# First expert table whole, then the second in groups of 4, 8, 8, 8 and 4 chunks, under one VectorE budget

## The chip, the core and the metric

One core of one Trainium2 chip runs the whole program. The metric is device time in microseconds from start to end of one execution; the times given are medians over runs, and the profile is of one execution of its own.

## What is computed

A decoder block on 256 tokens of width 2048 in float32: retention and dilated attention, a memory cross-attention, and then a PEER layer, in which every token picks 16 experts of 16384 for each of 8 heads. Only the last layer matters here:

```python
def peer_ffn(h, w_q, subkeys, u_tab, v_tab):
    qh = (ht @ w_q).reshape(t, PEER_HEADS, 2, PEER_QUERY_DIM // 2)
    sc = jnp.einsum('thpd,hpnd->thpn', qh, subkeys).astype(jnp.float32)
    v_top, i_top = lax.top_k(sc, PEER_TOPK)
    ...
    c_val, c_idx = lax.top_k(combo, PEER_TOPK)
    ...
    e_idx = i1 * PEER_N_KEYS + i2
    gates = jax.nn.softmax(c_val, axis=-1)
    ...
    def expert_block(args):
        x_, i_, g_ = args
        u = u_tab[i_]
        a = jax.nn.gelu(jnp.einsum('td,tkd->tk', x_, u), approximate=False)
        return jnp.einsum('tk,tkd->td', a * g_, v_tab[i_])
```

`u_tab` and `v_tab` have 16384 rows of 2048 floats each, 134 MB a table.

## The kernel before

Weights stream through the core as **pieces** of 128 x 4 x 512 floats (1 MB each). SP loads a piece into `raw` (three buffers, L1134); ScalarE casts it to the fp32r high part `hi` (L1144) and VectorE subtracts for the low part `lo` (L1145); TensorE multiplies with both. This split runs two pieces ahead of the matmuls. There are 464 pieces; the last 256 are the PEER tables, 128 of `u` and 128 of `v`. 32 chunks of 512 experts make a table, 4 pieces a chunk.

For 192 of the 256 tokens the layer is computed densely: all activations against `u` (`u_chunk`, L206 to L208, L900, L901; 20 matmuls of 512 columns a piece), times a gate matrix that is zero outside of the chosen experts, times `v` (`v_group`, 20 matmuls a piece, L1002, L1003). For the last 64 tokens the chosen rows are gathered instead ("lanes"): 128 gathered tiles of `u` rows and 128 of `v` rows, each 128 x 1024 floats (0.52 MB), fetched by an indirect DMA that POOL issues (L824), dotted on VectorE (L835) and later added up with weights on VectorE (L853). A fetch is written three tiles ahead of its use.

Beside the stream run generators, each a background job that gives up control with `yield`:

- `route`: the top-16 searches (L655 to L659), the pairs, the index picks (L712 to L715), all on VectorE, for one block of tokens and then for the other. Then `gate_matrix`: 24 batches of 8 tokens. Each token needs a weighted one-hot row (L751) and a plain one-hot row (L753), both on VectorE, and their outer product on TensorE (L760), which ScalarE copies out (L761) and SP writes to DRAM (`G`).
- `lanes`: the gathered rows.
- `weigh`: reads a chunk of `G` and of the activations back, multiplies (L939, L951), transposes, and splits the result (L945, L946, L959, L960) for `v_group`.

What sets the order is `tick()`. It is called once after a piece, and twice in a `u` piece while `fine` is set, from the start of `u` to the end of `gate_matrix`. Each generator has a credit of its own: `FINE` = 1.5 units a tick in the fine part, `TICK` = 4 outside; a yield names the cost of what was written. `lanes` yields 0.8 of two fine ticks' credit, or of one coarse tick's, and so advances 1.25 tiles a piece whatever else runs.

The stream takes the first 20 chunks of `u` (`RUN_AHEAD`), and then, in turn, a group of two chunks of `v` (8 pieces) and two chunks of `u`, until `u` is used up. At the end of each group, for each of four column blocks, `evac` adds both PSUM banks to the result rows in two VectorE adds (L969, L971).

Of the kernel before, what the change touches and what calls it, by code (L numbers as in the profile page):

```python
# [28 lines left out]
TOPK = 16  # L29
N_EXP = N_KEYS * N_KEYS  # L30
N_CH = N_EXP // 512
RUN_AHEAD = 20
RAW_BUFS = 3
SPLIT_AHEAD = 2
N_UNITS = 30
LANES = slice(64, 128)
LOW = slice(0, 64)
TICK = 4.0
LANE_STEP = 0.8
ROWS_AHEAD = 3  # L40
FINE = 1.5

P2PI = 2.0 * math.pi

# [31 lines left out]
def block_kernel(ctx, tc, a, out):  # L76
# [34 lines left out]
    nc.vector.tensor_copy(iota, iota_i)  # L111
    ident = cp.tile([128, 128], F32, name="ident")
    nc.vector.tensor_scalar(ident, diag_i, 0.0, None, op0=OP.is_equal)
    nhalf = cp.tile([128, 16], F32, name="nhalf")
    nc.vector.memset(nhalf, -0.5)
    warm = cp.tile([128, 1], F32, name="warm")
# [6 lines left out]

    def tick():

        gain = FINE if fine[0] else TICK
        for g in list(active):
            credit[g] = min(credit[g], 0.0) + gain
            try:
                while credit[g] > 0.0:  # L130
                    credit[g] -= next(g) or gain
            except StopIteration:
                active.remove(g)

    credit = {}

    def add(g):
        active.append(g)
        credit[g] = 0.0
        return g  # L140

    def wait(cond):
# [10 lines left out]
    def call(fn):  # L153
        prog.append((None, fn))
# [506 lines left out]
    G_d = [dp.tile([128 - 64 * tb, N_EXP], F32, name=f"G{tb}") for tb in range(2)]  # L661
    g_done = []

    rt = [{}, {}]

    def route_top(n, tb):

# [52 lines left out]
    def route_gates(tb):  # L720
        yield
        yield
        ex, sel, uc = rt[tb]["g"]
        nc.scalar.activation(ex, ex, AF.Exp)
        su = sp.tile([128, 2, 8], F32, tag="gsum", name="gsum")
        nc.vector.tensor_reduce(su[:, 0], ex, axis=AX.X, op=OP.add)
        nc.vector.reciprocal(su[:, 1], su[:, 0])
        nc.vector.tensor_tensor(sel[:, 2], ex, bc(su[:, 1, :, None], [128, 8, 16]), op=OP.mult)
        yield
        if tb:  # L730
            add(lanes(uc[:, 0:3]))
# [3 lines left out]
        nc.scalar.copy(uc[:, 3:6], tp)  # L735
        rt[tb] = {"T": uc[:, 3:6]}
        yield

    def gate_matrix():

        prev = None
        for tb, t0 in [(1, t0) for t0 in range(0, 64, 8)] + [(0, t0) for t0 in range(0, 128, 8)] + [(None, None)]:
            cur = None
            if tb is not None:
                it = rt[tb]["T"]
                cur = unit([8, 128]), unit([8, 128])
                for i in range(8):
# [50 lines left out]
    def lanes(sel):  # L800
# [26 lines left out]
        def turn():  # L827
            return LANE_STEP * (2 * FINE if fine[0] else TICK)
# [12 lines left out]
        ys = [unit([2, 512]) for _ in range(2)]  # L841
        for n in range(4):
# [7 lines left out]
        for i in range(128):  # L850
            r = rows.pop(128 + i)
            y = ys[i % 2].rearrange("p a b -> p (a b)")
            nc.vector.scalar_tensor_tensor(y, r, coef[:, i // 2:i // 2 + 1], y, op0=OP.mult, op1=OP.add)  # L853
            del r
            fetch(128 + i + ROWS_AHEAD)
            yield turn()
        for q in range(2):
            z = unit([2, 512])
            nc.scalar.copy(z[LANES], ys[q][LOW])
# [51 lines left out]
    def weigh():  # L911
# [18 lines left out]
        yield  # L930
        load(0)
        for c in range(N_CH):
            while (c + 1 < N_CH and c + 1 not in ga) or c > 2 * v_at[0] + 3:
                yield
            if c + 1 < N_CH:
                load(c + 1)
            yield
            t = w.pop(c)
            nc.vector.tensor_mul(t[:, 1], t[:, 1], t[:, 0])  # L939
            yield  # L940
# [6 lines left out]
            A_T[c] = o  # L947
            if c % 2 == 0:
# [3 lines left out]
            yield  # L952
# [10 lines left out]
    def v_group(gi):  # L963
        accs = {}
        last = gi == N_CH // 2 - 1

        def evac(n, acc):
            r = x_rows[n]
            nc.vector.tensor_add(r[:, 0], r[:, 0], acc[0])  # L969
            if not last:  # L970
                nc.vector.tensor_add(r[:, 1], r[:, 1], acc[1])  # L971
                if gi == N_CH // 2 - 2:
# [3 lines left out]
                    wait(lambda: "ys" in sm)  # L976
                    nc.scalar.copy(r[LANES, 1], sm["ys"][n // 2][LANES, n % 2])
                return
            w = work([512])
            nc.scalar.copy(w[LOW], acc[1][LANES])  # L980
            nc.vector.tensor_add(r[LOW, 1], r[LOW, 1], acc[1][LOW])
# [6 lines left out]
                    nc.gpsimd.tensor_mul(y_rows[n][:, tb], r[:, tb], g_fin[n // 2][:, n % 2])  # L988

        for n in range(4):  # L990
            for c2 in range(2):
                def fn(hi, lo, n=n, c2=c2):
                    c = 2 * gi + c2
                    v_at[0] = gi
                    wait(lambda: c in A_T and gi in B_T)
                    if c2 == 0:
                        accs[n] = [bank("acc", [512]) for _ in range(2)]
                    ta, tb = A_T[c], B_T[gi][:, c2]
                    for k in range(4):
                        f, e = c2 == 0 and k == 0, c2 == 1 and k == 3  # L1000
                        mm3(accs[n][0], ta[:, 0, k], ta[:, 1, k], hi[:, k], lo[:, k], f, e)
                        nc.tensor.matmul(accs[n][1], tb[:, k], hi[:, k], start=f, stop=False)  # L1002
                        nc.tensor.matmul(accs[n][1], tb[:, k], lo[:, k], start=False, stop=e)  # L1003
                    if n == 3:
                        del A_T[c]
                        if c2:
                            del B_T[gi]
                    if c2 == 1:
                        evac(n, accs.pop(n))
                piece(a["v"][(gi * 4 + n) * 2 + c2], fn)  # L1010


    g_fin = {}
# [86 lines left out]
            yield from route_gates(tb)  # L1100
        yield from gate_matrix()
    call(lambda: add(route()))
    call(lambda: add(weigh()))
    call(lambda: add(lanes_in()))

    def side_by_side(kq):
# [14 lines left out]

    stream = [e for e in prog if e[0] is not None]
# [113 lines left out]
def _layout(inputs):  # L1236
# [15 lines left out]
        "v": g["peer_v"][0].reshape(N_CH // 2, 2, 4, 128, 4, 512).transpose(0, 4, 1, 3, 2, 5).reshape(-1, 128, 4, 512),  # L1252
    }
    r.update(_constants())
    return {k: np.ascontiguousarray(v) for k, v in r.items()}
# [15 lines left out]
```

## Time and profile before

| | us |
|---|---|
| median of 3 runs (2646.44 to 2647.83) | 2647.04 |
| profiled execution | 2646.55 |
| its span, first to last instruction | 2644.8 |
| last split ahead of the `u` table to the last split of all | 1226.67 to 2622.40 |

The span is what the instructions show; 1.75 us of the profiled execution lie outside of it. In the views below, "busy" is the time in which an engine had an instruction under way; the granted clock of TensorE is a share of its full speed; instructions are named by the line that records them. Consecutive VectorE instructions overlap by some 0.08 us, so that the distance between two starts, not the duration, is what one costs in a row.

### The profile page before, as it was taken

What the parts mean: (1) busy time and instruction counts of PE and PEld (TensorE: products, weight loads), DVE (VectorE), ACT (ScalarE), POOL (GpSimd) and SP (SyncE); (2) the same over time, 40 slices, a digit from 0 to 9 for tenths busy, and PEclk for the clock granted to TensorE, in tenths of its full rate; (3) what the DMA queues carried; (4) which work ended last, traced back from release to release, by engine and by line L of the source; (5) the groups of instructions that cost most, each with busy time, mean ns of one, the idle gap of its engine ahead of it and who ended that gap; (6) DMA issues with size and microseconds to landing.
All of it is one profiled execution on the core that took longest, in us unless ns stands there. A gap on an engine that the chain in (4) does not pass through costs nothing.

```text
span 2644.8 us, 29732 instructions
## 1 busy us (share of the span) xinstructions
PE 2524.7 (95%) x11426; PEld 2077.2 (79%) x11426; DVE 1964.3 (74%) x2446; ACT 1176.3 (44%) x1084; POOL 573.1 (22%) x361
## 2 busy tenths in 40 slices
PE   9999999999999999999977799999999999899998
PEld 7888888888888888888765577778777878777786
DVE  7566546777564344556989999789888989899976
ACT  6444334443454443445433344454444444344444
POOL 0211110001000000000022233354443445355001
PEclk9999999999999999999998899999999999999999
DMA  7555555566575544564676799999999999999874
GB/s 288 201 181 170 181 193 172 179 237 245 207 284 177 191 155 148 178 220 163 207 278 237 250 291 301 337 374 398 393 366 347 394 383 416 361 381 388 302 267 153
DMA packets 160142, 700.51 MB, mean 265 GB/s; under 512 B 15968, under 2 KB 40576, under 8 KB 101120
## 3 DMA queue, kind: packets, MB, share of 16 engines
q1 hardware_dynamic: 110352, 531.18, 56.5%
q0 software_dynamic: 42736, 154.85, 15.5%
q10 hardware_dynamic: 6912, 12.59, 1.3%
q8 instruction: 90, 1.47, 0.2%
q14 instruction: 52, 0.43, 0.0%
HBM read 666.01 MB, written 31.98 MB: 264 GB/s over the span
## 4 chain that ended last, share of the span: by engine, by line
PE 50%; DVE 20%; DMA 7%; issue 5%; ACT 3%; POOL 0%; SPq 0%; ACTq 0%; DVEq 0%; POOLq 0%
PE acc L207 13%; PE acc L208 13%; PE acc L206 13%; DVE lo L1145 8%; DMA raw<-in_v_dram 3%; DVE unit L835 2%; ACT hi L1144 2%; PE acc L1002 2%; PE acc L1003 2%; DVE unit L751 2%; DVE unit L753 1%; DMA raw<-in_u_dram 1%; PE acc L900 1%; PE acc L901 1%; DMA unit<-in_v_rows_dram,unit 1%
## 5 line engine op out<-in xcount | busy, mean ns | idle before, releaser
L1145 DVE TENSOR_TENSOR lo<-raw,hi 128x2048 fp32r<-128x2048 f32 (+1 forms) x464 | 1058.7, 2283 | 508.4 <-ACT hi L1144 502.3
L1144 ACT CAST hi<-raw 128x2048 fp32r<-128x2048 f32 (+1 forms) x464 | 877.7, 1900 | 658.6 <-PE acc L208 292.9
L207 PE MATMUL acc<-lo,unit 128*128 128x512 f32 x2688 | 1059.1, 394 | 34.1 <-DVE lo L1145 33.6
L206 PE MATMUL acc<-hi,unit 128*128 128x512 f32 x2688 | 1069.4, 398 | 15.9 <-ACT hi L1144 9.7
L208 PE MATMUL acc<-hi,unit 128*128 128x512 f32 x2688 | 1054.4, 392 | 0.0
L207 PEld LDWEIGHTS acc<-lo,unit 128*128 128x128 f32 x2688 | 510.2, 190 | 149.4 <-DVE lo L1145 47.9
L206 PEld LDWEIGHTS acc<-hi,unit 128*128 128x128 f32 x2688 | 510.0, 190 | 120.3 <-ACT hi L1144 12.2
L208 PEld LDWEIGHTS acc<-hi,unit 128*128 128x128 f32 x2688 | 509.5, 190 | 106.3
L824 POOL DMA_INDIRECT unit<-in_u_rows_dram,unit x128 | 226.1, 1766 | 379.1 <-DVE unit L835 173.2
L824 POOL DMA_INDIRECT unit<-in_v_rows_dram,unit x128 | 241.1, 1883 | 251.3 <-DVE unit L853 64.5
L900 PE MATMUL acc<-hi,unit 128*128 128x512 f32 x512 | 204.2, 399 | 0.0
L901 PE MATMUL acc<-lo,unit 128*128 128x512 f32 x512 | 203.6, 398 | 0.0
L1002 PE MATMUL acc<-hi,unit 128*128 128x512 f32 x512 | 200.6, 392 | 0.0
L1003 PE MATMUL acc<-lo,unit 128*128 128x512 f32 x512 | 200.4, 391 | 0.0
L853 DVE SCALAR_TENSOR_TENSOR unit<-unit 128x1024 f32<-128x1024 f32 x128 | 161.5, 1277 | 6.8 <-DMA unit<-xs 6.7
L835 DVE CUSTOM_DVE_ANT_0 unit<-unit 128x1024 f32<-128x1024 f32 x128 | 154.6, 1216 | 4.8 <-DMA unit<-in_u_rows_dram,unit 4.7
L900 PEld LDWEIGHTS acc<-hi,unit 128*128 128x128 f32 x512 | 99.2, 194 | 21.7
L901 PEld LDWEIGHTS acc<-lo,unit 128*128 128x128 f32 x512 | 99.0, 193 | 21.5
L1003 PEld LDWEIGHTS acc<-lo,unit 128*128 128x128 f32 x512 | 96.7, 189 | 20.6
L1002 PEld LDWEIGHTS acc<-hi,unit 128*128 128x128 f32 x512 | 96.7, 189 | 20.6
L760 PE MATMUL sm<-unit 128*128 128x128 f32 x384 | 62.9, 309 | 13.8 <-DVE unit L753 9.5
L338 POOL TENSOR_TENSOR unit<-work 128x512 f32<-128x512 f32 x20 | 37.8, 1888 | 176.4 <-DVE work L336 157.0
(233 smaller groups left out, 1435.8 us busy)
## 6 DMA issues: line engine op xcount, KB each, us to landing
raw<-in_u_dram SPq DMA_DIRECT2D x128, 1024.0 KB
raw<-in_v_dram SPq DMA_DIRECT2D x128, 1024.0 KB
raw<-in_w_in_dram SPq DMA_DIRECT2D x96, 1024.0 KB
raw<-in_w_kv_dram SPq DMA_DIRECT2D x32, 1024.0 KB
raw<-in_w_out_dram SPq DMA_DIRECT2D x16, 1024.0 KB
raw<-in_w_qm_dram SPq DMA_DIRECT2D x16, 1024.0 KB
raw<-in_w_om_dram SPq DMA_DIRECT2D x16, 1024.0 KB
raw<-in_w_pq_dram SPq DMA_DIRECT2D x16, 1024.0 KB
```

What stands on the lines that cost most here:

```text
L206: nc.tensor.matmul(acc, lh, rh, start=start, stop=False)
L207: nc.tensor.matmul(acc, lh, rl, start=False, stop=False)
L208: nc.tensor.matmul(acc, ll, rh, start=False, stop=stop)
L824: nc.gpsimd.indirect_dma_start(rows[i], None, t, bass.IndirectOffsetOnAxis(ap=ix[:, j // 2, j % 2:j % 2 + 1], axis=0))
L835: nc.vector.tensor_tensor_reduce(r, r, hn[i % 2].rearrange("p a b -> p (a b)"), 1.0, 0.0, OP.mult, OP.add, dots[:, i // 2, i % 2:i % 2 + 1])
L853: nc.vector.scalar_tensor_tensor(y, r, coef[:, i // 2:i // 2 + 1], y, op0=OP.mult, op1=OP.add)
L900: nc.tensor.matmul(accs[1], th[:, k, 128:256], hi[:, k], start=first, stop=False)
L901: nc.tensor.matmul(accs[1], th[:, k, 128:256], lo[:, k], start=False, stop=last)
L1002: nc.tensor.matmul(accs[n][1], tb[:, k], hi[:, k], start=f, stop=False)
L1003: nc.tensor.matmul(accs[n][1], tb[:, k], lo[:, k], start=False, stop=e)
L1144: nc.scalar.copy(hi[:, ks], raw[:, ks])
L1145: nc.vector.tensor_sub(lo[:, ks], raw[:, ks], hi[:, ks])
```

## The change

- The stream takes all 32 chunks of `u` first and then `v` in five groups of 4, 8, 8, 8 and 4 chunks. The input `v` is laid out in that order. A group of 8 holds its two PSUM banks over 8 pieces for each column block, and there are 5 times 4 evacuations in place of 16 times 4. `hf_T` is given up at the end of `u`.
- `tick()` has one budget for all generators in the PEER part, to its end: 1.3 units, twice a piece, in `u` and in `v`. Generators are served by rank: `route` (and `lanes_in`) first, then `weigh`, then `lanes`. Lanes cost 1.28 units a tile, a half batch of one-hots 1.1, the steps of `weigh` 0.7 to 0.8.
- The plain one-hots go from VectorE to ScalarE, as Relu(1 - (iota - index) squared): eight Squares of 128 columns and one Relu of 1024 a batch. The indices are kept negated, and the weighted one-hots on VectorE compare with a negated iota.
- The chunk limit of `weigh` follows the chunks that are used up, 3 ahead in `u` and 9 ahead in `v`. The copy of `ys` moves to the last group.

```diff
-RUN_AHEAD = 20
+V_GROUPS = (4, 8, 8, 8, 4)
...
-LANE_STEP = 0.8
...
-FINE = 1.5
+BUDGET = 1.3
...
+        if fine[0]:
+            left[0] = min(left[0], BUDGET) + BUDGET
+            for g in sorted(active, key=lambda g: rank.get(g, 0)):
+                try:
+                    while left[0] > 0.0:
+                        cost = next(g)
+                        if not cost:
+                            break
+                        left[0] -= cost
+                except StopIteration:
+                    active.remove(g)
+            return
...
-                    nc.vector.tensor_scalar(cur[0][:, i], iota, it[:, 0, t], it[:, 2, t],
+                    nc.vector.tensor_scalar(cur[0][:, i], niota, it[:, 0, t], it[:, 2, t],
                                             op0=OP.is_equal, op1=OP.mult)
-                    nc.vector.tensor_scalar(cur[1][:, i], iota, it[:, 1, t], None, op0=OP.is_equal)
+                    nc.scalar.activation(cur[1][:, i], iota, AF.Square, bias=it[:, 1, t])
+                    if i % 4 == 3:
+                        yield 1.1
+                nc.scalar.activation(cur[1], cur[1], AF.Relu, scale=-1.0, bias=rt["one"])
...
-            yield 2.6
-        fine[0] = False
+            yield 0.1
...
-            yield turn()
+            yield 1.28
...
-            while (c + 1 < N_CH and c + 1 not in ga) or c > 2 * v_at[0] + 3:
+            while (c + 1 < N_CH and c + 1 not in ga) or c > v_at[0] + (3 if hf_T[0] is not None else 9):
...
+            wait(lambda: "ys" in sm)
+            nc.scalar.copy(r[LANES, 1], sm["ys"][n // 2][LANES, n % 2])
...
-    for c in range(RUN_AHEAD):
+    for c in range(N_CH):
         u_chunk(c)
-    for gi in range(N_CH // 2):
-        if gi == N_CH // 2 - 1:
+    def end_u():
+        hf_T[:] = [None] * 4
+    call(end_u)
+    c0 = 0
+    for gi, count in enumerate(V_GROUPS):
+        if gi == len(V_GROUPS) - 1:
             call(load_g_final)
-        v_group(gi)
-        for c in range(RUN_AHEAD + 2 * gi, min(RUN_AHEAD + 2 * gi + 2, N_CH)):
-            u_chunk(c)
+        v_group(gi, c0, count)
+        c0 += count
```

Three places show what this makes of the order. On VectorE, the beginning of one piece in the routing of the second token block, before (L1145 is the split of a piece; a top-16 search is the five rows from MAX to MAX_INDEX; L835 is the dot of one gathered tile, in two rows):

```order
L1145 TENSOR_TENSOR lo<-raw,hi 128x2048
L655 MAX unit<-unit 128x8
L656 MAX_INDEX unit<-unit 128x8
L657 MATCH_REPLACE work<-unit 128x128
L658 MAX unit<-work 128x8
L659 MAX_INDEX unit<-unit,work 128x8
L835 ISA unit<-unit 128x1024
L835 ISA unit 128x1
```

The same routing with the change, from one split to the next:

```order
L1172 TENSOR_TENSOR lo<-raw,hi 128x2048
L672 MAX unit<-unit 128x8
L673 MAX_INDEX unit<-unit 128x8
L674 MATCH_REPLACE work<-unit 128x128
L675 MAX unit<-work 128x8
L676 MAX_INDEX unit<-unit,work 128x8
L1172 TENSOR_TENSOR lo<-raw,hi 128x2048
```

The dot is gone from between the splits; the searches stay.

On ScalarE, two pieces in the building of the gate matrix, before (L1144 is the cast of a piece, L761 copies the products of four tokens):

```order
L1144 CAST hi<-raw 128x2048
L761 COPY unit<-sm 128x512 x2
L1144 CAST hi<-raw 128x2048
L761 COPY unit<-sm 128x512 x2
```

The same with the change (L774 Square of one token, L777 Relu of eight, L785 the copies):

```order
L1171 CAST hi<-raw 128x2048
L774 ACTIVATE unit<-iota,unit 128x128 x8
L777 ACTIVATE unit<-unit,one 128x1024
L785 COPY unit<-sm 128x512 x2
L774 ACTIVATE unit<-iota,unit 128x128 x4
L1171 CAST hi<-raw 128x2048
```

Eight to twelve Squares and a Relu came in beside each cast; on VectorE eight to twelve one-hots a piece remain.

On VectorE, two pieces some 80 pieces into the tables, before (L969 and L971 are the evacuation of a group's column block):

```order
L1145 TENSOR_TENSOR lo<-raw,hi 128x2048
L969 TENSOR_TENSOR unit<-unit,acc 128x512
L971 TENSOR_TENSOR unit<-unit,acc 128x512
L835 ISA unit<-unit 128x1024
L835 ISA unit 128x1
L1145 TENSOR_TENSOR lo<-raw,hi 128x2048
L835 ISA unit<-unit 128x1024
L835 ISA unit 128x1
```

The same place with the change:

```order
L1172 TENSOR_TENSOR lo<-raw,hi 128x2048
L855 ISA unit<-unit 128x1024
L855 ISA unit 128x1
L855 ISA unit<-unit 128x1024
L855 ISA unit 128x1
L1172 TENSOR_TENSOR lo<-raw,hi 128x2048
```

Two gathered tiles stand between two splits in place of 1.25 on average, and the evacuations are gone from there.

## Rows read from the trace of the kernel before

**Rows 1.** Page, part 1: busy us of each engine, share of the span, instructions.
```profile
PE 2524.7 (95%) x11426; PEld 2077.2 (79%) x11426; DVE 1964.3 (74%) x2446; ACT 1176.3 (44%) x1084; POOL 573.1 (22%) x361
```

**Rows 2.** Windows, five stages: us, busy PE, PEld, DVE, ACT, POOL, granted clock, DMA, GB/s.
```profile
1226.67:1543.58 316.91, 263.94 (x1099) 207.64 (x1098) 285.50 (x633) 129.76 (x111) 56.85 (x39) 0.92 0.69 239
1543.58:1723.77 180.19, 163.28 (x800) 136.24 (x799) 164.18 (x402) 79.43 (x83) 64.57 (x31) 0.93 0.95 309
1723.77:2001.82 278.05, 265.29 (x1168) 217.27 (x1166) 239.47 (x252) 128.82 (x96) 123.41 (x72) 0.98 0.99 378
2001.82:2433.38 431.56, 416.74 (x1857) 340.52 (x1856) 398.51 (x320) 193.07 (x140) 214.42 (x114) 0.99 1.00 387
2433.38:2622.40 189.02, 187.18 (x846) 153.79 (x844) 155.07 (x133) 93.77 (x78) 15.22 (x11) 1.00 0.75 266
```

**Rows 3.** Windows of the split L1145 alone, first and fourth stage: DVE busy (count).
```profile
1226.67:1543.58 316.91, 109.64 (x48) 0.92 0.69 239
...
2001.82:2433.38 431.56, 201.30 (x88) 0.99 1.00 387
```

**Rows 4.** Timeline of VectorE, one piece in the gate matrix: start, us, line.
```profile
1550.56 2.28 DVE L1145 TENSOR_TENSOR lo<-raw,hi 128x2048 fp32r<-128x2048 f32 x1
1552.76 0.33 DVE L751 TENSOR_SCALAR unit<-iota,unit 128x128 f32<-128x128 f32 x1
1553.02 0.27 DVE L753 TENSOR_SCALAR unit<-iota,unit 128x128 f32<-128x128 f32 x1
...
1556.38 1.21 DVE L835 CUSTOM_DVE_ANT_0 unit<-unit 128x1024 f32<-128x1024 f32 x1
...
1557.52 2.27 DVE L1145 TENSOR_TENSOR lo<-raw,hi 128x2048 fp32r<-128x2048 f32 x1
```

**Rows 5.** Timeline of TensorE, one batch of the gate matrix and the piece behind.
```profile
1547.46 2.57 PE L760 MATMUL sm<-unit 128*128 128x128 f32 x16
1549.79 0.48 PE L206 MATMUL acc<-hi,unit 128*128 128x512 f32 x1
...
1552.17 0.39 PE L206 MATMUL acc<-hi,unit 128*128 128x512 f32 x1
...
1553.30 0.39 PE L206 MATMUL acc<-hi,unit 128*128 128x512 f32 x1
```

**Rows 6.** Groups by line: busy us, mean ns of one, idle before.
```profile
L1144 ACT CAST hi<-raw 128x2048 fp32r<-128x2048 f32 x460 | 875.6, 1911 | 658.6 <-PE acc L208 292.9 <-DMA raw<-in_v_dram 148.0 <-DMA raw<-in_u_dram 73.0
L761 ACT COPY unit<-sm 128x512 f32<-128x512 f32 x48 | 27.7, 587 | 54.4 <-PE sm L760 49.7 <-issue 4.2 <-ACT unit L878 0.4
...
L261 ACT ACTIVATE unit<-unit 128x1024 f32<-128x1024 f32 x8 | 8.5, 1057 | 5.8 <-DMA unit<-in_x_dram 5.8
...
L432 ACT ACTIVATE work<-sm 128x128 f32<-128x128 f32 x16 | 4.3, 279 | 1.4 <-POOL unit L338 1.4
...
L824 POOL DMA_INDIRECT unit<-in_v_rows_dram,unit x128 | 241.1, 1883 | 251.3 <-DVE unit L853 64.5 <-PE tp L943 52.0 <-PE tp L955 47.6
```

**Rows 7.** Windows of 50 and of 10 us with the most DMA traffic.
```profile
2200.00:2250.00 50.00, 50.00 (x222) 41.39 (x221) 44.26 (x30) 24.94 (x17) 28.99 (x17) 1.00 1.02 417
...
1760.00:1770.00 10.00, 10.00 (x46) 8.28 (x45) 9.18 (x11) 5.19 (x3) 7.67 (x4) 1.00 1.02 420
2100.00:2110.00 10.00, 10.00 (x47) 8.26 (x47) 10.00 (x9) 4.23 (x3) 3.38 (x3) 1.00 1.01 404
```

**Rows 8.** Timeline of POOL, and of VectorE at the last of them.
```profile
2049.27 0.94 POOL L824 DMA_INDIRECT unit<-in_v_rows_dram,unit  x1 [0.30 <-issue]
...
2057.66 3.94 POOL L824 DMA_INDIRECT unit<-in_v_rows_dram,unit  x1 [0.66 <-DVE unit L853]
...
2058.50 2.28 DVE L1145 TENSOR_TENSOR lo<-raw,hi 128x2048 fp32r<-128x2048 f32 x1
```

**Rows 9.** Waits, who for whom: us, times, longest; third stage, then 1900:2000.
```profile
ACT hi L1144 <- DMA raw<-in_v_dram: 37.2, 11, 8.1
...
DVE unit L853 <- DMA unit<-xs: 6.7, 1, 6.7
```

More of the change, by code (lines that the diff above doesn't have):

```diff
@@ L113, in block_kernel @@
     nc.vector.tensor_scalar(ident, diag_i, 0.0, None, op0=OP.is_equal)
+    niota = cp.tile([128, 128], F32, name="niota")
+    nc.vector.tensor_scalar(niota, iota_i, -1.0, None, op0=OP.mult)
     nhalf = cp.tile([128, 16], F32, name="nhalf")
@@ L124, in tick, with add @@
     def tick():
-        gain = FINE if fine[0] else TICK
+        if fine[0]:
[10 more added lines that the diff above has]
+            return
         for g in list(active):
-            credit[g] = min(credit[g], 0.0) + gain
+            credit[g] = min(credit[g], 0.0) + TICK
             try:
                 while credit[g] > 0.0:
-                    credit[g] -= next(g) or gain
+                    credit[g] -= next(g) or TICK
             except StopIteration:
                 active.remove(g)
+    left = [0.0]
+    rank = {}
     credit = {}
-    def add(g):
+    def add(g, later=0):
         active.append(g)
         credit[g] = 0.0
+        rank[g] = later
         return g
@@ L662, in block_kernel @@
     g_done = []
-    rt = [{}, {}]
+    rt = {0: {}, 1: {}}
     def route_top(n, tb):
@@ L730, in route_gates @@
         if tb:
-            add(lanes(uc[:, 0:3]))
+            add(lanes(uc[:, 0:3]), 2)
         tp = bank("tp", [3, 128])
@@ L734, in route_gates @@
             nc.tensor.transpose(tp[:, s], uc[:, s], ident)
-        nc.scalar.copy(uc[:, 3:6], tp)
+        nc.scalar.activation(uc[:, 3:5], tp[:, 0:2], AF.Copy, scale=-1.0)
+        nc.scalar.copy(uc[:, 5], tp[:, 2])
+        if tb:
+            rt["one"] = cp.tile([128, 1], F32, name="one")
+            nc.vector.memset(rt["one"], 1.0)
         rt[tb] = {"T": uc[:, 3:6]}
@@ L825, in fetch @@
                     ap=ix[:, j // 2, j % 2:j % 2 + 1], axis=0))
-        def turn():
-            return LANE_STEP * (2 * FINE if fine[0] else TICK)
         for i in range(ROWS_AHEAD):
@@ L855, in lanes @@
             fetch(128 + i + ROWS_AHEAD)
-            yield turn()
+            yield 1.28
         for q in range(2):
@@ L939, in weigh @@
             nc.vector.tensor_mul(t[:, 1], t[:, 1], t[:, 0])
-            yield
+            yield 0.7
             tp = bank("tp", [4, 128])
@@ L947, in weigh @@
             A_T[c] = o
+            yield 0.7
             if c % 2 == 0:
@@ L951, in weigh @@
             nc.vector.tensor_mul(t[:, 1], t[:, 1], t[:, 0])
-            yield
+            yield 0.7
             tp = bank("tp", [4, 128])
@@ L961, in weigh, with v_group @@
             B_T[c // 2] = o
-    def v_group(gi):
+            yield 0.8
+    def v_group(gi, c0, count):
         accs = {}
-        last = gi == N_CH // 2 - 1
+        last = gi == len(V_GROUPS) - 1
         def evac(n, acc):
@@ L971, in evac @@
                 nc.vector.tensor_add(r[:, 1], r[:, 1], acc[1])
-                if gi == N_CH // 2 - 2:
+                if gi == len(V_GROUPS) - 2:
                     w = work([512])
@@ L975, in evac @@
                     nc.vector.tensor_add(r[LOW, 1], r[LOW, 1], w[LOW])
-                    wait(lambda: "ys" in sm)
-                    nc.scalar.copy(r[LANES, 1], sm["ys"][n // 2][LANES, n % 2])
                 return
+            wait(lambda: "ys" in sm)
+            nc.scalar.copy(r[LANES, 1], sm["ys"][n // 2][LANES, n % 2])
             w = work([512])
@@ L990, in v_group, with fn @@
         for n in range(4):
[L991 to L995, printed above, removed]
+            for c2 in range(count):
+                def fn(hi, lo, n=n, c=c0 + c2, c2=c2):
+                    wait(lambda: c in A_T and c // 2 in B_T)
                     if c2 == 0:
                         accs[n] = [bank("acc", [512]) for _ in range(2)]
-                    ta, tb = A_T[c], B_T[gi][:, c2]
+                    ta, tb = A_T[c], B_T[c // 2][:, c % 2]
                     for k in range(4):
-                        f, e = c2 == 0 and k == 0, c2 == 1 and k == 3
+                        f, e = c2 == 0 and k == 0, c2 == count - 1 and k == 3
                         mm3(accs[n][0], ta[:, 0, k], ta[:, 1, k], hi[:, k], lo[:, k], f, e)
@@ L1003, in fn @@
                         nc.tensor.matmul(accs[n][1], tb[:, k], lo[:, k], start=False, stop=e)
+                        if k == 1:
+                            tick()
                     if n == 3:
                         del A_T[c]
-                        if c2:
-                            del B_T[gi]
-                    if c2 == 1:
+                        v_at[0] += 1
+                        if c % 2:
+                            del B_T[c // 2]
+                    if c2 == count - 1:
                         evac(n, accs.pop(n))
-                piece(a["v"][(gi * 4 + n) * 2 + c2], fn)
+                piece(a["v"][4 * c0 + n * count + c2], fn)
     g_fin = {}
@@ L1102, in block_kernel @@
     call(lambda: add(route()))
-    call(lambda: add(weigh()))
+    call(lambda: add(weigh(), 1))
     call(lambda: add(lanes_in()))
@@ L1251, in _layout @@
         "u": g["peer_u"][0].reshape(N_CH, 512, 4, 4, 128).transpose(0, 2, 4, 3, 1).reshape(-1, 128, 4, 512),
-        "v": g["peer_v"][0].reshape(N_CH // 2, 2, 4, 128, 4, 512).transpose(0, 4, 1, 3, 2, 5).reshape(-1, 128, 4, 512),
+        "v": np.concatenate([
+            g["peer_v"][0][512 * c0:512 * (c0 + n)].reshape(n, 4, 128, 4, 512).transpose(3, 0, 2, 1, 4).reshape(-1, 128, 4, 512)
+            for c0, n in zip(np.cumsum((0,) + V_GROUPS), V_GROUPS)]),
     }
```

## The prediction

> **What bounds the kernel now.** I read the busy sums first [rows 1]: TensorE is busy 95% of the span, so the kernel looks bound by it. The sum hides five different stages, so I cut the PEER part by the splits of its 256 pieces [rows 2, 3] into 48, 24, 56, 88 and 40 pieces. A piece is 20 matmuls of 512 columns. Two L206 with five matmuls from the one to the other start 1.13 us apart in a run without gaps [rows 5], 0.227 us a matmul, so a piece needs 4.53 us of TensorE. What each stage gets:
>
> - Stage A (routing, first gate batches): 316.9 us for 48 pieces, 6.6 us each. VectorE is busy 285.5 us of it, TensorE 263.9 at a granted clock of 0.92, that is, partly at 1.2 and mostly at 2.4 GHz after gaps [rows 2]. VectorE sets the pace.
> - Stage B (most of the gate matrix): 180.2 us for 24 pieces, 7.5 us each. In its core a piece takes 6.97 us on VectorE without a gap: the split, eight pairs of one-hots, a dot [rows 4]. TensorE is nearly as full: a batch of the gate matrix takes it 2.33 us [rows 5], with a piece's 4.53 us that is 6.86.
> - Stages C and D (56 and 88 pieces, with the gathered tiles): 4.97 and 4.90 us a piece. TensorE is busy 95 and 97%, the DMA share is 0.99 and 1.00 at 378 and 387 GB/s [rows 2]. ScalarE's casts wait for loads here, 37 us in stage C for pieces of `v` alone [rows 9], though mostly within the two pieces of lead.
> - Stage E (40 pieces, gathered tiles nearly done): 4.73 us a piece, TensorE busy 99% [rows 2]. It is TensorE's own pace.
>
> **The change, part by part.** I go stage by stage; the order shows that the same 48, 24, 56, 88 and 40 pieces keep the routing, the gate matrix and the gathered tiles in the same stages, only with other numbers of them.
>
> Stage A. The order has 33 dots and 5 batches of one-hots there before, and 3 dots and no batch with the change; the routing is the same. A dot costs VectorE 1.14 us from start to start (1556.38 to 1557.52), a pair of one-hots 0.45 (3.62 us from 1552.76 to 1556.38 for eight) [rows 4]. VectorE loses 30 x 1.14 = 34 us and 40 x 0.45 = 18 us. 316.9 - 52 = 265 us stays above TensorE's 48 x 4.53 = 218 plus some 6 of transposes and scores, so VectorE still sets the pace and all of it counts: **-52 us**. If half of the remaining 31 us of VectorE's idle time grows, because the waits between softmax and transposes are no longer filled with dots, it is -40.
>
> Stage B. All 24 batches are in it now (19 before), and no dot until its end. VectorE needs 2.2 + 9 x 0.26 = 4.5 us a piece and is out of the way. TensorE needs 24 x 4.53 + 24 x 2.33 = 165 us. ScalarE takes over the plain one-hots: no row has a Square with these operands, the nearest is L432 with 0.279 us for 128 columns; the Relu is like L261, 1.057; two copies at 0.587 [rows 6]. 8 x 0.279 + 1.057 + 1.174 = 4.46 us a batch, 107 for 24; casts 24 x 1.91 = 46, the evacuations of six chunks some 11 (three instructions of 512 columns each, about 0.6 apiece): 164 us, as much as TensorE. These are durations, and starts stand a little closer, so TensorE is the bound by a small margin. Before, no engine was busy for more than 164 of the 180 us [rows 2]; with two engines equally full I take 175: **-5 us**, from -12 (TensorE alone) to +15 (Squares at 0.35).
>
> Stages C and D. What leaves VectorE: 88 of 124 evacuation adds, 53 us at about 0.6 (a quarter of the split's 2.2 and a start), but mostly where TensorE is busy 95 to 99%. What comes: the tiles that stage A and B had. Stage C gets 108 tiles instead of 69, stage D 135 instead of 110. The traffic: a piece is 1.049 MB, a tile 0.524, a chunk of activations written 0.39 on average, a chunk of `weigh` 0.52 plus half as much for the last tokens. Stage C before: 58.7 + 36.2 and 8 of the rest = 103 MB, and 103 MB in 278 us is 370 GB/s, which agrees with the view's 378. With the change: 58.7 + 56.6 + 8.2 = 123.5 MB. Stage D before: 165 MB (383 GB/s, the view 387); with the change 92.3 + 70.8 + 21.2 = 184.3 MB. The highest 10 us windows show 420 GB/s, and 417 is held for 50 us with a DMA share of 1.02 [rows 7]: I read this as the ceiling. Two tiles and a piece are 2.1 MB; at 417 GB/s that is 5.03 us, more than TensorE's 4.53 and than VectorE's 2.2 + 2 x 1.14 + 0.15 = 4.65. So **DMA becomes the bound of both stages**. I take 412 GB/s, near the rows at 404 to 420: C = 123.5 / 0.412 = 300 us, **+22**; D = 184.3 / 0.412 = 447, and 7 for the turn to the `v` rows, which waits for `xs` now [rows 9] and will again: 454, **+23**. At 420 the two are +16 and +14; at stage D's own 387, taken as the most that a mix can have, +41 and +52.
>
> The Trainium skill has two other figures for this ceiling ("DMA: Bandwidth & Descriptors", Specifications): about 358 GB/s from HBM to one core, and 435 for the fabric. By 358 the two stages would take 860 us, 150 more than now, and the kernel would be slower; the trace does not agree, since 50 us at 417 stand there [rows 7]. By 435 they would cost some 5 us, estimated from that page.
>
> Stage E. 6 tiles instead of 14, 88 fewer adds in all, none of it on TensorE's path: 40 x 4.53 and a few transposes is 186 of 189: **-3**.
>
> Costed at nothing: the negated iota and the constant (two small VectorE instructions, ahead of work that waits for loads or in the routing), the split copy in `route_gates` (one more ScalarE instruction, twice), the layout of `v` (same size, contiguous as before), the chunk limit of `weigh` (by the order, each chunk's parts stand 8 or more pieces ahead of their first use, 40 us). The `ys` copy stands now in the last group, ahead of the last sums: about 0.6 us of ScalarE in the tail, **+1**.
>
> Sum: 2644.8 - 52 - 5 + 22 + 23 - 3 + 1 = 2630.8 us of span, 2632.5 with the 1.75 us around it, and the medians lie 0.5 above the profiled run: **2633 us**, 0.5% faster.
>
> **The rivals.**
>
> *No DMA ceiling.* If the plateau at 417 is only demand, VectorE sets the pace in C and D: by the order's counts, 262 and 419 us of VectorE work, with 2% and the turn 267 and 434: -11 and +2. The sum is 2645 - 52 - 5 - 11 + 2 - 3 + 1 = 2577 of span, 2579 as a median. For it: TensorE is at full pace in the very windows at 417. Against it: the flat top, with a share of 1.02.
>
> *POOL cannot issue two tiles a piece (slower).* An indirect DMA takes POOL 0.94 us alone and 3.94 when it meets VectorE's long instructions: it ends 0.82 us after the split at 2058.50 has ended [rows 8]. The mean is 1.88, 2.18 with the 0.30 between two [rows 6, 8], and 16 tiles in 8 pieces need 35 us of 43. It decides from 2.67 us a tile. VectorE is denser in two-input instructions with the change; if each tile took 3.2 us (2.9 and 0.3), stage C would take 108 x 3.2 = 346 us, 46 more than forecast, and the 65 tiles of D's dense stretches 208 instead of 164: 2633 + 90 = 2723. The Trainium skill says why ("SBUF — State Buffer", Terms: VectorE and GpSimd lock a shared port pair for a whole instruction, the loser blocks); the trace agrees.
>
> *ScalarE is late in stage B.* Its 164 us become 187 if a Square takes 0.40 us: with 5% on top 196, +16 instead of -5, 2654, a little slower.
>
> **How the numbers follow.** About 0.2%, 5 us, can be told from no change here. Forecast (DMA ceiling between 395 and 420; the kernels are equal at about 403): 0.67, of which 0.48 faster, 0.09 the same, 0.10 slower. No ceiling: 0.14, faster. POOL: 0.11, slower. ScalarE: 0.08, half the same, half slower. Faster 0.62, same 0.13, slower 0.25. The range goes from 2574, which takes in the no-ceiling case, to 2680, which takes in 387 GB/s (2679) and the milder half of POOL's case.
>
> **What would show it.** Stage A at 260 to 275 us with no L855 between the searches, and a granted clock above 0.92. Stage B at 168 to 190 with TensorE and ScalarE both above 85%. Stages C and D at 405 to 420 GB/s with TensorE below 90% busy, dots or casts waiting for DMA. If they run at 4.7 us a piece with more than 425 GB/s, the ceiling is wrong; if POOL is busy throughout and DMA below 390, POOL is the bound; if stage A does not fall, something other than VectorE paced it.

## The result, and the profile after

The changed kernel takes 2736.74 us (median of 4, 2736.20 to 2740.41), the kernel before 2646.74 beside it: a ratio of 1.0347, 95% interval 1.0329 to 1.0365. It is **3.5% slower**; the forecast was 2633 us, faster, with a range to 2680. Both its sign and its range were wrong.

The busy sums of the page, part 1 (busy us, share of the span, instructions), beside [rows 1]:

```profile
PE 2541.2 (93%) x11426; PEld 2083.6 (76%) x11426; DVE 1880.1 (69%) x2168; ACT 1254.9 (46%) x1302; POOL 541.5 (20%) x361
```

VectorE has 84 us less to do, as the change wants, and the kernel is 90 us longer. The five stages, cut at the same splits as in [rows 2] (us; busy PE, PEld, DVE, ACT, POOL; granted clock, DMA share, GB/s):

```profile
1226.75:1498.39 271.64, 244.59 (x1041) 195.19 (x1040) 232.92 (x494) 128.94 (x114) 7.98 (x8) 0.97 0.62 212
1498.39:1682.35 183.96, 159.11 (x842) 137.33 (x841) 114.54 (x234) 157.53 (x297) 7.36 (x5) 0.93 0.81 249
1682.35:1985.35 303.00, 276.23 (x1166) 219.57 (x1165) 266.41 (x297) 136.71 (x106) 181.10 (x112) 0.98 1.00 399
1985.35:2516.40 531.05, 444.49 (x1900) 353.68 (x1899) 427.74 (x359) 191.34 (x144) 237.06 (x134) 0.94 0.93 350
2516.40:2710.45 194.05, 186.86 (x810) 153.87 (x809) 119.14 (x77) 90.53 (x69) 12.00 (x9) 0.97 0.64 227
```

| stage, us | before | forecast | after |
|---|---|---|---|
| A, routing | 316.9 | 265 | 271.6 |
| B, gate matrix | 180.2 | 175 | 184.0 |
| C, tiles in `u` | 278.1 | 300 | 303.0 |
| D, tiles in `v` | 431.6 | 454 | 531.1 |
| E, end of `v` | 189.0 | 186 | 194.1 |

A is 7 us late and C 3, B and E are 8 to 9 us late, and D is 77 us late: three quarters of the miss. D has lost its clean signature: before, TensorE was busy 97% at a DMA share of 1.00 [rows 2]; now it is 84%, and DMA, at 0.93, is not full either. Who waits for whom in D (us in all, times, longest):

```profile
ACT hi L1171 <- DMA raw<-in_v_dram: 121.6, 37, 7.0
ACT unit L965 <- PE tp L963: 114.9, 26, 9.8
...
PE tp L963 <- DVE unit L959: 69.8, 24, 8.8
```

L959 is the multiplication of `weigh` on VectorE, L963 its four transposes on TensorE, L965 the copy on ScalarE. On the page's list of groups these transposes have 86 us of idle TensorE ahead of them in the whole program; before, the wait for the same step (then PE L943 for DVE L939) was 12.5 us in all:

```profile
L963 PE MATMUL tp<-ident,unit 128*128 128x128 f32 x128 | 23.1, 309 | 86.0 <-DVE unit L959 86.0
```

One such wait on the timeline of TensorE in D (start, length; in brackets the idle time ahead):

```profile
2427.01 0.40 PE L1023 MATMUL acc<-lo,unit 128*128 128x512 f32 x1
2436.12 1.08 PE L963 MATMUL tp<-ident,unit 128*128 128x128 f32 x4 [8.72 <-DVE unit L959]
2436.86 0.78 PE L223 MATMUL acc<-hi,unit 128*128 128x512 f32 x1
2437.43 0.63 PE L224 MATMUL acc<-lo,unit 128*128 128x512 f32 x1
...
2441.27 0.63 PE L223 MATMUL acc<-hi,unit 128*128 128x512 f32 x1
2441.70 0.56 PE L224 MATMUL acc<-lo,unit 128*128 128x512 f32 x1
2442.10 0.39 PE L225 MATMUL acc<-hi,unit 128*128 128x512 f32 x1
2442.33 0.40 PE L1022 MATMUL acc<-hi,unit 128*128 128x512 f32 x1
```

and VectorE over the same time:

```profile
2428.49 2.29 DVE L1172 TENSOR_TENSOR lo<-raw,hi 128x2048 fp32r<-128x2048 f32 x1
2430.69 2.48 DVE L873 SCALAR_TENSOR_TENSOR unit<-unit 128x1024 f32<-128x1024 f32 x2
2433.08 2.29 DVE L1172 TENSOR_TENSOR lo<-raw,hi 128x2048 fp32r<-128x2048 f32 x1
2435.28 0.69 DVE L959 TENSOR_TENSOR unit<-unit 128x512 f32<-128x512 f32 x1
2437.86 0.69 DVE L966 TENSOR_TENSOR unit<-tp,unit 128x512 fp32r<-128x512 f32 x1 [1.89 <-ACT unit L965]
```

VectorE is not idle in the 8.7 us. It works through two splits and two tiles that stand ahead of L959 in its order, and TensorE, whose next instruction in its own order is the transposes, can't go on with pieces that are already split. Then VectorE waits in turn, 1.89 us, for the copy. In the old `weigh` the empty `yield` between multiplication and transposes put a whole piece between the two, for all 48 multiplications; the new one says `yield 0.7`, and a budget of 1.3 a tick lets it go on within the same tick.

### The profile page after: what moved, and what is told of

Read it like the earlier page. It is cut to its first block, busy times and chain, and to the rows that moved or that the text cites. A ratio compares the mean times of both kernels' runs of the same rounds, so it can differ in the third digit from the quotient of the medians.

```text
span 2734.3 us, 29754 instructions
## 1 busy us (share of the span) xinstructions
PE 2541.2 (93%) x11426; PEld 2083.6 (76%) x11426; DVE 1880.1 (69%) x2168; ACT 1254.9 (46%) x1302; POOL 541.5 (20%) x361
## 4 chain that ended last, share of the span: by engine, by line
PE 44%; DVE 14%; DMA 10%; issue 10%; ACT 7%; POOL 2%; ACTq 0%; SPq 0%; DVEq 0%; POOLq 0%
PE acc L224 12%; PE acc L225 12%; PE acc L223 12%; DVE lo L1172 7%; ACT hi L1171 3%; DMA unit<-in_u_rows_dram,unit 3%; DMA unit<-in_v_rows_dram,unit 3%; DMA unit<-act 2%; PE acc L1022 2%; PE acc L1023 2%; ACT unit L774 1%; POOL unit L847 1%; DVE unit L855 1%; DMA raw<-in_u_dram 1%; DVE unit L873 1%
## 5 line engine op out<-in xcount | busy, mean ns | idle before, releaser
L847 POOL DMA_INDIRECT unit<-in_v_rows_dram,unit x128 | 231.6, 1810 | 281.4 <-DVE unit L873 104.0
L847 POOL DMA_INDIRECT unit<-in_u_rows_dram,unit x128 | 203.9, 1593 | 319.7 <-DMA G<-unit 151.1
L963 PE MATMUL tp<-ident,unit 128*128 128x128 f32 x128 | 23.1, 309 | 86.0 <-DVE unit L959 86.0
L963 PEld LDWEIGHTS tp<-ident,unit 128*128 128x128 f32 x128 | 15.3, 155 | 98.0 <-issue 69.2
```

## The experiments

Times are medians; stages are cut at the same splits. The number in a label gives the order of the runs. e3_thin, e4_vec, e8_thinall, e15_pairsthin and e16_eventhin were run once each.

Three terms: *adjacency* is that the transposes of `weigh` stand right behind their own multiplication; *bursts* are steps of `weigh` that come close together and then not at all; the *trip* is ScalarE's way to VectorE and back in `evac_u`, the end of a `u` chunk.

**Two empty yields put back** (e1_gap). After each multiplication of `weigh` in the kernel after:

```
+            yield
+            yield
             tp = bank("tp", [4, 128])
```

> The changed kernel, with one edit: two empty yields (one piece of the stream) between the multiplication of a chunk in weigh and its transposes, as far apart as they were before. Theory W (the matmul queue stands still at each transpose, because VectorE reaches the multiplication only then, and so the two pieces of lead are lost once a chunk): the 88 pieces of stage D fall from 531 to 450-465 us, stage E by 8-10, TensorE's idle time ahead of the weigh transposes from 86 us to under 25; total 2640-2660. Theory P (POOL or DMA cannot deliver the gathered tiles in stage D): D stays above 510 and the total above 2715.

Measured: 2692.5 us (1.0174 of before, 1.0148 to 1.0200), D 498.4, C 299.0, E 190.8. 44 us come back, 33 of them in D: half of what theory W asked. TensorE's idle time ahead of the L959 transposes falls from 86 to 35 us in the whole program, not to under 25. D in e1_gap:

```profile
1978.38:2476.75 498.37, 436.00 (x1874) 349.97 (x1873) 428.30 (x355) 190.35 (x139) 233.04 (x134) 0.94 0.98 372
```

**The yields taken out of the kernel before** (e2_nogap), the mirror of it:

> The kernel before, with the two yields between multiplication and transposes of weigh taken away, so that both stand in one step as in the changed kernel. Theory W: each chunk costs 2 to 3 us where the gathered tiles are under way, 48 multiplications: 2690-2760, with TensorE idle 60 us or more ahead of the weigh transposes. If the distance does not matter (theory P, or the changed order of the tables), 2640-2655.

Measured: 2752.35 us, 1.0406 (1.0373 to 1.0439). The two lines alone cost 106 us, with the old order of tables and the old tile rate: B +12, C +7, D +56, E +27. The waits of TensorE in the whole program show the step (in this kernel L942 and L953 are the two sets of transposes, L939 and L950 the multiplications):

```profile
PE tp L942 <- DVE unit L939: 62.7, 25, 5.3
PE tp L953 <- DVE unit L950: 38.2, 16, 3.8
```

Before they were 12.5 and 13.4. That adjacency costs TensorE this much is shown from both sides.

**Gathered rows a quarter as wide** (e3_thin), as many transfers; the kernel leaves out the other three quarters of each row:

> The changed kernel, with gathers of 256 columns in place of 1024 (a quarter of the bytes, the same number of indirect DMAs; VectorE reads the same 256 columns four times over, so the lanes' part of the result is left out). Read in stage C, 56 pieces, 303 us now. If the DMA rate of 413 GB/s sets C: 262-272 us. If POOL's issue of two tiles a piece sets it: 295-305. Stage D keeps its weigh stalls: 88 pieces at about 495-515 with theory W, since its undisturbed pieces go from 5.1 to 4.7 us; total 2655-2690.

Measured: 2709.3 us, C 295.7, D 515.4. C hardly moved, with the DMA share down to 0.81:

```profile
1681.00:1977.00 296.00, 273.91 (x1167) 220.16 (x1166) 265.49 (x299) 137.43 (x106) 183.65 (x112) 0.98 0.81 272
```

So bytes are not alone in C. The time is the one that the expectation gave to POOL, but POOL is busy for only 184 of the 296 us. The timeline shows a trip once a chunk: ScalarE copies (L899), VectorE adds (L900) behind two dots and the split between them, ScalarE's Gelu waits for it, and the next cast waits behind the Gelu:

```profile
1862.55 0.69 DVE L900 TENSOR_TENSOR work<-work,acc 64x512 f32<-64x512 f32 x1
...
1863.27 0.72 ACT L901 ACTIVATE unit<-work,rstdB 64x512 f32<-64x512 f32 x1 [4.94 <-DVE work L900]
...
1864.39 3.71 ACT L1174 CAST hi<-raw 128x2048 fp32r<-128x2048 f32 x2 [0.40 <-ACT unit L901]
```

**Plain one-hots back on VectorE** (e4_vec), the rest as in the kernel after:

> The changed kernel, with the plain one-hots back on VectorE (Squares and Relu away), the budget as it is. Stage B, 24 pieces, 184 us now: with ScalarE as its bound (2.45 us of Squares and 1.15 of Relu a batch, 86 us in all) it falls to 170-176; with TensorE as its bound (165 us) it stays at 180-190; with VectorE (2.2 us + 9 pairs at 0.45 a piece = 6.3) it is no slower either. Everything else as it is: total 2722-2740.

Measured: 2723.7 us, B 173.4. ScalarE held B by 10.6 us, though it was busy only 157.5 of 184.

**`weigh` taken apart** (e5_pipe). Multiplication, transposes and subtraction of different chunks side by side, with pieces between them:

```
+            if due(turned, 1):
+                low()
...
+            if due(fresh, 2) and len(turned) < 3:
+                flip()
...
+                    nc.vector.tensor_mul(t[:, 1], t[:, 1], t[:, 0])
+                    fresh.append((t, part, c, at["split"]))
```

> The kernel after with `weigh` taken apart: a chunk's multiplication, its transposes (two pieces later) and its subtraction (one more piece later) are written for different chunks side by side, and chunks may run 11 ahead instead of 9, so that nothing VectorE writes is needed by TensorE or ScalarE sooner than two pieces on. Theory W (the whole loss of stage D over the forecast is this coupling): D falls from 531 to 440-460 us, E to about 190, the kernel to 2640-2665 us, and TensorE's idle time ahead of the transposes of `weigh` is under 10 us. Rival (the run with two empty yields left D at 498 because two gathered tiles a piece or the bursts cost it by themselves): D stays above 480, the kernel above 2680.

Measured: 2729.9 us, D 537. Neither theory: the coupling had only changed its form. The transposes now waited for the subtraction two steps earlier, which still had to read the PSUM bank that they write:

```profile
PE tp L958 <- DVE unit L974: 41.1, 16, 7.5
```

**The second Gelu of `evac_u` a piece later** (e6_late), behind the next cast:

```
+        owed.append((c, d, b, w, own))
+
+    def settle():
...
         nc.scalar.activation(b[own], w[own], AF.Gelu, scale=sm["rstdB"][own])
```

> The kernel after; in `evac_u` the second Gelu (the one that waits for VectorE's addition) is written one piece later, behind ScalarE's next cast. Theory R (the trip ScalarE copy, VectorE addition behind two dots, ScalarE Gelu, next cast, once a chunk, paces stage C): C falls from 303 to 265-285 us, which needs 430 to 460 GB/s. Rival, the DMA ceiling of the prediction (412 GB/s, at most 420): C stays at 292-303 us. The other stages stay within 3 us of those of the kernel after: 2710-2737 us in all by R, 2726-2737 by the ceiling.

Measured: 2721.85 us (1.0279); C 305.1. C is two above the end that the ceiling gave, and theory R fell: with whole rows the DMA share was 0.99, and the trip can at most be the next limit behind it. What nobody had forecast is A, 271.6 to 257.9 us. There the Gelu waits for VectorE behind the searches, 30.7 us now and, in the kernel after, 51.0:

```profile
ACT unit L898 <- DVE work L897: 51.0, 11, 7.3
```

**Both, and the one-hots on VectorE** (e7_all):

> Both edits above together, and the plain one-hots back on VectorE: W with the DMA ceiling gives B 174, C 293-303, D 440-460 and 2625-2650 us; W without a ceiling C 265-285, D 420-440 and 2580-2615; if both fall, more than 2680.

Measured: 2694.3 us: A 257, B 163, C 300, D 534. Both theories fell in D; the fault of e5_pipe is in it too.

**e5_pipe and e6_late with the narrow rows** (e8_thinall):

> Both edits, with the gathered rows fetched a quarter as wide (256 of 1024 columns, as many transfers; the last 64 tokens' layer output is left wrong): nothing is bound by bytes here. VectorE's own sums then bound C at 262-275 and D at 420-440 us. If C and D come out as in the runs with whole rows, bytes bound nothing there, and the forecast's DMA ceiling falls; if they come out 20 us or more below those, the ceiling stands. POOL issues as many transfers as before: if C stays at 295, POOL or VectorE is the pace.

Measured: 2656.6 us, C 295.2, D 498.3 (the fault of e5_pipe is in D). C stays at 295 with neither bytes nor the trip. By its occupancy POOL is the pace here: in 1735 to 1945 us 84 fetches took it 2.40 us each, 180 of 210 us, and 22 more went by between two issues. At 2.70 us in all, 16 tiles take 43 us, and 8 pieces of this C take 42. The mean of the fetches of `v` before was 1.88 [rows 6]. One of the fetches, with the one ahead of it:

```profile
1855.56 0.95 POOL L847 DMA_INDIRECT unit<-in_u_rows_dram,unit  x1 [0.30 <-issue]
1856.81 13.78 POOL L847 DMA_INDIRECT unit<-in_u_rows_dram,unit  x1 [0.30 <-issue]
```

From 1855.62 to 1869.8 VectorE ran without a gap, three splits and six dots; the fetch ended 0.8 us after that. It lasted nearly three times as long as the longest fetch in the kernel before (5.07 us, at 1556.10). The Trainium skill ("SBUF — State Buffer", Terms) says that VectorE and GpSimd lock a shared port pair for a whole instruction. The row agrees in that the fetch is held until VectorE pauses, but it is held over nine instructions, which that sentence alone doesn't give. Nor is a VectorE without gaps enough: from 1838.67 to 1855.58 it had none either, and the fetches at 1848.86, 1851.07 and 1853.35 took 1.91 to 1.98 us. What decides between the two is not shown. The slower rival of the prediction is real, then, but in C it stands behind DMA, and comes out when bytes and trip are gone.

**`weigh` taken apart, with four PSUM banks instead of two** (e9_pipe4):

> The pipelined `weigh` of e5_pipe, which left D at 537 us, with the two faults that its trace shows mended: four PSUM banks instead of two (its transposes waited for the subtraction that reads the same bank), and chunks 9 ahead as in the kernel after, so that fewer buffers are held. Tiles still at two a piece. Theory W: D 440-465, E 183, the kernel 2640-2665 us. Rival, the supply (two tiles a piece leave the split without a lead over TensorE, whatever `weigh` does): D stays above 480 and C at 300, the kernel above 2675.

Measured: 2692.6 us, D 501, C 302. TensorE's waits for transposes fell to 21 us in D, and D is where e1_gap has it. W alone doesn't reach the forecast.

**Fewer tiles a piece** (e10_gaprate): e1_gap with a tile at 1.6 units.

> The kernel of e1_gap (2692.5 us) with one number changed: a gathered tile costs 1.6 units of the budget instead of 1.28, so that 13 tiles come in 8 pieces instead of 16, and the rest in the last stage. Theory of the supply: with 13 tiles TensorE is the bound again (8 pieces then take 36.3 us of it; bytes 15.2 MB, 37 us at 412 GB/s; POOL 13 x 2.7 = 35 us), the lead of two pieces comes back, and the one piece between multiplication and transposes is enough: C falls from 299 to 270-285, D from 498 to 435-465, E rises from 191 to 190-205, the kernel to 2600-2650 us. Rival (only the coupling counts, and tiles cost nothing until a ceiling): C and D within 10 us of e1_gap, 2680-2700 us.

Measured: 2667.2 us (1.0083, 1.0062 to 1.0104), C 274.5, D 492.3, E 199.3. C fell as forecast, D did not. The order shows why that is no contradiction: the tiles that C gave up went to D, and D's to E, so that D still has 134 of them.

**All that the runs pointed to so far** (e11_best):

> All that the runs point to: the pipelined `weigh` of e9_pipe4 (at 0.5 units a step), the later second Gelu, the plain one-hots on VectorE, and a tile at 1.6 units. A 257, B 163-170, C 260-285, D 420-445, E 185-195: 2530-2600 us, faster than both kernels. If C and D stay above 290 and 480, neither supply nor coupling is what holds them.

Measured: 2636.6 us, 0.9962 (0.9948 to 0.9976), a little faster than before; D still 500. In D VectorE waited 68.8 us for reads of the activations that were issued one step ahead of their multiplication.

**Groups of two chunks** (e12_pairs), as before, in e1_gap:

```
-V_GROUPS = (4, 8, 8, 8, 4)
+V_GROUPS = (2,) * 16
```

> The kernel of e1_gap (2692.5 us, D 498) with the second table in 16 groups of two chunks, as in the kernel before, instead of 4, 8, 8, 8, 4; nothing else. Chunks are then used up two in eight pieces all along, so the steps of `weigh`, 12 in some 9 pieces and then none for 23, come 3 in every 8 pieces; tiles fall to 11-13 in 8 pieces with the same sum over D. Theory of the bursts (reloads of 0.79 MB a chunk in bursts on top of pieces and tiles pass what DMA moves, and TensorE is idle meanwhile, while it is full in between): D falls from 498 to 435-455 us, E 186-192, the kernel to 2625-2655. Rival (the new order of tables or the shared budget holds D by itself): D above 480, the kernel above 2670.

Measured: 2690.6 us, D 499.2 against 498.4. This theory fell: D does not change. Groups of two also bring 64 more VectorE instructions into D (419 for 355, 30 us of work), so what is shown is that the two together cost nothing beside the groups of the change, and that these groups are not what D lost.

**Groups of two, `weigh` apart and paced** (e13_even):

> The kernel of e11_best with the second table in 16 groups of two and at least two pieces between two steps of `weigh`. Theory of the bursts: A 256, B 165, C 275, D 400-425, E 183-192, the kernel 2520-2560 us, 3 to 5% faster than the kernel before. Rival: D above 480 as in e11_best, 2620 us or more.

Measured: 2612.2 us, 0.9875 (0.9858 to 0.9892): faster than both kernels by 34 and 124 us. A 256, B 165, C 272, D 473, E 195. D is better than in e11_best, and not at the 400 to 425 hoped for. VectorE's wait for the reads in D fell from 68.8 to 17.4 us; whether groups or pace did it was not taken apart.

**Groups of two in the kernel after, transposes next to the multiplication** (e14_after2):

> The kernel after with the second table in 16 groups of two and nothing else, so that transposes stay next to their multiplication. If bursts and adjacency are two causes that add, D lands between: 531 less the 45-60 of the bursts, 470-490 us, the kernel 2680-2700. If adjacency alone is enough to hold TensorE, D stays above 510; if bursts alone mattered, D falls below 460.

Measured: 2751.05 us, D 549.8. It differs from e12_pairs by the empty yields alone, and D by 51 us: adjacency again.

```profile
1984.34:2534.12 549.78, 452.89 (x1911) 366.71 (x1910) 462.14 (x419) 192.87 (x145) 264.98 (x133) 0.91 0.93 338
```

**Narrow rows on e12_pairs and on e13_even** (e15_pairsthin, e16_eventhin), to see whether DMA binds D:

> The kernel of e12_pairs (D 499 us at a DMA share of 0.99 and 374 GB/s, C 300 at 1.01 and 403) with the gathered rows a quarter as wide, as in e3_thin (the layer's result for the last 64 tokens is left wrong). Theory of the rate (D is bound by DMA time, only at 375 GB/s instead of the forecast's 412): D falls to 430-460 us at a share under 0.85. Rival (the one piece between multiplication and transposes is too little once the splits have no lead, and the share of 0.99 is only queueing): D stays at 480-500.

> The same thinning on e13_even (D 473 us at 0.99 and 377 GB/s, C 272 at 402), where `weigh` is decoupled. Theory of the rate: D 400-425 us, C 255-268. Rival: D above 455.

Measured: D 475.4 and 440.2 us, C 290.3 and 252.7. D by stage windows, e12_pairs, e13_even, and the two with narrow rows:

```profile
1977.80:2476.97 499.17, 440.82 (x1919) 349.94 (x1919) 458.41 (x419) 190.74 (x145) 244.08 (x134) 0.97 0.99 374
```

```profile
1918.95:2392.27 473.32, 437.30 (x1924) 348.50 (x1923) 435.14 (x422) 189.99 (x143) 240.64 (x121) 0.98 0.99 377
```

```profile
1963.86:2439.30 475.44, 432.66 (x1918) 345.36 (x1917) 457.63 (x419) 190.78 (x145) 239.20 (x135) 0.99 0.80 277
```

```profile
1893.30:2333.50 440.20, 429.41 (x1935) 346.59 (x1934) 433.71 (x421) 192.52 (x145) 281.90 (x119) 1.00 0.84 295
```

With whole rows DMA is full (0.99) and D falls when bytes go: by 24 and 33 us. Both lie above the range that the theory gave, because right below DMA stands VectorE, busy 96 and 99% in the narrow runs. So in these two kernels DMA binds D once adjacency is gone, by 24 to 33 us over VectorE, and not by more. e1_gap was not run with narrow rows.

## Why the prediction was wrong

**D, first step that failed: costed at nothing, "the chunk limit of `weigh` (by the order, each chunk's parts stand 8 or more pieces ahead of their first use, 40 us)".** I looked at how far each part stands ahead of its first use by the matmuls, and not at how far the transposes stand behind their own multiplication. The prediction has no term for that distance, which `yield 0.7` in place of the empty `yield` took from a piece to none. In D it costs 33 us (e1_gap) to 51 (e14_after2 against e12_pairs), in the whole kernel 44 to 60, and in the kernel before 106.

**D, second step: the rate of 412 GB/s.** The peak windows [rows 7] hold pieces and tiles. D also reads G and activations back, in rows of 2 KB, and the change moves most of these reads into D (26 chunks instead of 16, by DMA's list of issues). The forecast had their 21.2 MB, at the rate of the rest. The DMA queues in D, before and in e12_pairs (q1: pieces and what `weigh` reads; q0: tiles; packets, MB, share of 16 engines):

```profile
q1 hardware_dynamic: 19695, 104.73, 63.2%
q0 software_dynamic: 16258, 59.21, 34.8%
```

```profile
q1 hardware_dynamic: 24464, 113.52, 60.5%
q0 software_dynamic: 19823, 72.16, 37.5%
```

and in C of the kernel after, where q1 is nearly all pieces:

```profile
q1 hardware_dynamic: 8800, 59.25, 48.8%
```

The traces hold each packet with its size and time. Added up by size and shared among the 16 engines, they give what a MB cost in us of DMA time:

| | pieces, 8 KB | tiles, 4 KB | read back, 2 KB |
|---|---|---|---|
| forecast (412 GB/s) | 2.43 | 2.43 | 2.43 |
| 2200 to 2250 us before [rows 7] | 2.40 | 2.46 | none |
| C, after | 2.47 | 2.48 | 3.21 |
| D, before | 2.53 | 2.52 | 3.06 |
| D, e1_gap | 2.58 | 2.56 | 3.04 |
| D, e12_pairs | 2.58 | 2.58 | 2.96 |

In D of e12_pairs the pieces took 238 us, the tiles 186, the reads 62 and small packets some 6, 492 in all, where the forecast had 447. Of the 45 us, 14 are the pieces' price, 11 the tiles' and 11 that of the reads; the rest are the small packets and a little more data. So the reads are dearer than the pieces beside them by a sixth to a fifth, but most of the loss is that pieces and tiles cost more here than in the best window. Why they do is open. The prices are not fixed either: with narrow rows a piece costs 2.87 in D (e15_pairsthin).

The share times the length of D says the same of every version with these tiles: 0.93 x 531 = 494 after, 0.98 x 498 = 488 in e1_gap, 0.99 x 499 = 494 in e12_pairs. In e13_even, with 121 fetches in D instead of 134, it is 469, and D is 473. I had D's own 387 GB/s, at a share of 1.00, before me [rows 2], and used it only for the end of the range; by it D would have been 476, and 483 with the turn. (With it the whole comes to 2681 us, not the 2679 of the prediction, just past the end that was to take it in.) The mechanism (DMA becomes D's bound) comes out right once the distance is back; its price was 40 us too small.

e1_gap divides the 77 us: 33 come back with the distance, and 44 stay (498 - 454). That these 44 are DMA time is worked out from the rows; that DMA binds D at such a length is shown by the two narrow runs, on kernels close to e1_gap.

**C** came out at 303 for 300, at 399 GB/s (the sign was 405 to 420) and a share of 1.00, for the forecast's reason: with 13 tiles in 8 pieces instead of 16 it is 274.5 (e10_gaprate), and with the bytes gone too and the trip removed 252.7 (e16_eventhin). The forecast did not see that other limits stood within 8 us behind (the trip in `evac_u` by the timeline of e3_thin, POOL by its occupancy in e8_thinall), so that narrow rows or a later Gelu alone gave no more than some 7 us. (In the prediction's sum for VectorE there, 2.2 + 2 x 1.14 + 0.15 is 4.63 and not 4.65; nothing hangs on it.)

**A** was 271.6 for 265. That VectorE's searches set the pace was right as far as it went, and the granted clock rose from 0.92 to 0.97; 14 us hung on the Gelu that waits behind them (e6_late).

**B** was 184 for 175. The rival named ScalarE with Squares of 0.40 us. ScalarE was indeed the holder (e4_vec: 173.4), busy 86% of the stage, and a Square does last 0.40 us; but Squares overlap and fill only 0.31 us each (57.3 us for 183). So its busy sum came out at 157.5, under the 164 that I had added up, and it was not the price of its instructions that failed but the step from "two engines equally full" to -5. Which of its waits makes the difference I did not take apart.

**E** rose by 5 instead of falling by 3: a last set of `weigh` steps falls into it, with 7 us of TensorE's waits for it, and in e9_pipe4, with `weigh` taken apart, E is 181.75.

**The chances.** The slower rival (POOL) was not the cause, though a run shows it at 2.4 us a fetch when bytes and trip are gone. No rival had the cause that counted, a distance in the order that shrank. The order shows it plainly, VectorE's multiplication and TensorE's transposes in the same half piece; the prediction looked there for first uses only.

## What to carry to other kernels

When engines work in order, read the distance between producer and consumer in both engines' orders after any change of a scheduler, at every step between them and at every buffer that is reused, not just at the last use: in this kernel one piece of distance is worth 44 to 106 us. Take a transfer rate from the mix of the stage that will have it, not from the best window. Where several limits stand within a few per cent of each other, an edit that removes the first shows the second; add up every engine's work and DMA time for the stage before believing in one.

## What the hardware showed that I had not expected

- A fetch on POOL can be held over many VectorE instructions: 13.78 us in e8_thinall, where the longest price in the prediction was 3.94 [rows 8]. All six fetches of over 10 us in that run start within 1.3 us of `evac_u`'s addition on VectorE (L899); others got through in 1.9 us under VectorE work as dense.
- Reads in rows of 2 KB (those of `weigh`) took 2.96 to 3.06 us of DMA time a MB in D, where pieces took 2.53 to 2.58. A piece's own price depends on what runs beside it: 2.47 in C of the kernel after, and 2.82 in its E, where hardly anything else is under way.
- A stall costs TensorE more than its length: after the 8.72 us at 2427, matmuls start 0.43 us apart until 2441.70, at a granted clock of 0.50 (1.2 GHz), and 0.23 from 2442.10 on, at 1.00 (2.4 GHz), as ahead of the stall. Twelve matmuls at 0.20 us more are 2.4 us; the granted clock of D fell from 0.99 before to 0.94.
